# Written issue order on four engines for four column chunks of the first layer, and sliding attention in smaller steps

## The chip, the cores and the metric

The kernel runs on one NeuronCore of a Trainium2 chip. The core has a matrix engine (PE, with its weight loads shown as PEld), a vector engine (DVE), an activation engine (ACT), a general engine (POOL) and a queue engine (SP) that issues the DMA transfers here. The engines run beside each other; each takes its own instructions in order, and semaphores make one wait for another. The metric is device time in microseconds (us), the median of several executions; a profile is one execution, taken apart by the hardware profiler.

## What is computed

Two layers of a hybrid block on a sequence of 256 tokens (two blocks of 128, called t = 0 and t = 1) with 1024 channels, all in float32:

```
h = rms_norm(x)
z = h @ w_in                 # retention, conv, gated MLP, sliding attention and gate columns
ya = retention(za);  yb = conformer_conv(zb)
yc = spatial_gating(zc);  yd = swa_attention(zd)
mix = sum_b sigmoid(g_b) * (y_b @ w_branch[b])
x = x + mix @ w_out
x = x + swiglu(rms_norm(x))
```

The sliding attention has 8 query heads of width 64 that share 2 key and value heads. A token sees the 128 latest tokens, so block 0 meets 128 keys and block 1 meets 256. Scores get a bias and a sink term, then a softmax, then the product with the values.

## The kernel before

**Products.** Weights come in units of 2 x 128 x 1024 numbers, each half by one DMA (`load`, L121) into one of six buffers. `part` splits a half into a rounded main part `wh` (a cast on ACT, L129) and the rest `wl` (a subtraction on DVE, L130); there is room for four units of each. `mm` then does three matrix products per block of 128 rows: L152 (main by main), L153 (main by rest), L154 (rest by main). One column chunk (`chunk`) is 512 columns of `w_in` for both token blocks: two units, hence two half chunks of 24 products each. Taking the units of a chunk (`take`, `ahead`) first writes out the cast and subtraction of the units up to two ahead.

**PSUM.** Products of chunks go to four `acc` banks, everything else (transposes, scores, attention output) to four `mid` banks. A bank comes free when ACT or DVE has read it.

**Side work in steps.** The mixers are generators. `spawn` runs one to its first `yield`; `tick`, called after each half chunk, runs each waiting generator to its next `yield`. So side work is written into the program between half chunks of products. Below, T1, T2, ... are the ticks of `columns`, counted in each layer: chunk `pa` (first half of the convolution input) has T1 and T2, `pg` (its gate) T3 and T4, `pq` (retention queries) T5 and T6, `pk` (keys) T7 and T8, `pv` T9 and T10.

**Sliding attention.** For a token block: `swa_sums` (squares on ACT L460 and L461, sums on DVE, the inverse root on POOL L205), `swa_scaled` (DVE L475, L481), `swa_qkT` (transposes on PE L188 and L493, a copy of the queries on ACT L495, of the keys on DVE L496), `swa_soft` (score products L513; bias and row maximum on DVE L520 to L530; eight exponentials on ACT L534 with their sums; sum and reciprocal on DVE L537, L538; eight scalings on ACT L540), `swa_pT` (eight transposes L547 and two ACT copies L550 for one key block), `swa_pv` (L557) and `emit_y` (ACT L195, DVE L197). In the first layer, scores, scaling and transposes of block 0's queries up to `swa_qkT` are already done in `opening`.

**Order.** Instructions outside `manual_schedule` are put in order by a list scheduler that goes by its own estimates of time; inside it, the engines named take theirs in the order of the program. `opening` names PE, ACT, DVE and POOL (`ORDERED`). In `columns`, of either layer, the chunks `pa` to `pv` name PE alone. SP is never named; single DMAs are pinned to program order.

Of the kernel before, what the change touches and what calls it, by code (L numbers as in the profile page):

```python
# [2 lines left out]

# [5 lines left out]
F32 = mybir.dt.float32  # L9
BF16 = mybir.dt.bfloat16  # L10
F32R = mybir.dt.float32r
AF = mybir.ActivationFunctionType
# [4 lines left out]
P = 128  # L17
D = 1024
T = 2
# [63 lines left out]
class Kernel:  # L83
# [414 lines left out]
        )  # L498
        self.sqT[t] = qT

    def swa_soft(self, t):
        nc = self.nc
        nk = P * (t + 1)
        b0 = 256 - nk
        sc = self.b8.tile([P, 8, nk], F32, tag="b8", name="sc")
        mx = self.small("mx", 8)
        qT = self.sqT[t]
        for j0 in (0, 2):
            banks = [self.bank() for _ in range(2)]
            for j in (j0, j0 + 1):  # L510
                for v in range(2):
                    r = slice(64 * v, 64 * v + 64)
                    nc.tensor.matmul(  # L513
                        banks[v][:, (j - j0) * nk : (j - j0 + 1) * nk],
                        qT[r, j * P : (j + 1) * P], self.skT[r, 0:nk], start=True, stop=True,
                    )
            for j in (j0, j0 + 1):
                for v in range(2):
                    h = 4 * v + j
                    nc.vector.tensor_tensor_reduce(  # L520
                        out=sc[:, h, :], in0=banks[v][:, (j - j0) * nk : (j - j0 + 1) * nk],
                        in1=self.bias[:, h, b0:256], scale=1.0, scalar=NEG,
                        op0=ALU.add, op1=ALU.max, accum_out=mx[:, h : h + 1],
                    )
        nm = self.small("nm", 8)
        sk = self.col[:, C_SK : C_SK + 8]
        nc.vector.tensor_tensor(out=mx, in0=mx, in1=sk, op=ALU.max)
        nc.vector.tensor_scalar(out=nm, in0=mx, scalar1=-1.0, scalar2=None, op0=ALU.mult)
        es = self.small("es", 8)
        nc.vector.tensor_tensor(out=es, in0=sk, in1=mx, op=ALU.subtract)  # L530
        nc.scalar.activation(es, es, AF.Exp)
        den = self.small("den", 8)
        for h in range(8):
            nc.scalar.activation(  # L534
                sc[:, h, :], sc[:, h, :], AF.Exp, bias=nm[:, h : h + 1], accum_out=den[:, h : h + 1]
            )
        nc.vector.tensor_tensor(out=den, in0=den, in1=es, op=ALU.add)  # L537
        nc.vector.reciprocal(den, den)  # L538
        for h in range(8):
            nc.scalar.activation(sc[:, h, :], sc[:, h, :], AF.Copy, scale=den[:, h : h + 1])  # L540
        return sc

    def swa_pT(self, sc, pT, kb):
        for h0 in (0, 4):
# [189 lines left out]
                op0=ALU.add, op1=ALU.mult,  # L734
            )

    def chunk(self, act, pool=None):
        units = self.take(2)
        ps = [self.abank() for _ in range(T)]
        for i, u in enumerate(units):  # L740
            for t in range(T):
                self.cols(act, t, [u], ps[t], 4 * i)
            self.tick()
        return ps

# [9 lines left out]
        for _ in gen:  # L755
            pass

    def swa_task(self, t, psq, pskv, first=False):
        if not (first and t == 0):
            qk = self.swa_scaled(t, psq, pskv, *self.swa_sums(t, psq, pskv))  # L760
            for _ in range(1 + t):
                yield
            self.swa_qkT(t, *qk)
        yield
        sc = self.swa_soft(t)
        for _ in range(2 if first or t == 0 else 3):
            yield
        pT = self.b8.tile([P, t + 1, 8, P], F32, tag="b8", name="pT")
        self.swa_pT(sc, pT, 0)
        yield  # L770
        if t:
            self.swa_pT(sc, pT, 1)
            yield
        self.emit_y(3, t, self.swa_pv(t, pT), 1.0)

    def emit_y(self, b, t, src, scale):
# [2 lines left out]
        self.Y[b, t] = self.yt[b][:, t]  # L779
        self.split(self.Y[b, t], 0, src, scale)  # L780

    def conv_task(self, pa, pg):
        us = [self.conv_gate(pa[t], pg[t]) for t in range(T)]
        yield
        for t in range(T):
            self.conv_uT(t, us[t])
        yield
        k = 0
        per = TAP_PLAN
        for n in per:  # L790
            self.conv_taps(k, k + n)
            k += n
            yield
        st = [self.conv_norm(t) for t in range(T)]
        yield
        cn = [self.conv_scale(*st[t]) for t in range(T)]
        yield
        for t in range(T):
            self.conv_act(t, cn[t])

    def rot_task(self, ps, i):
        rs = [self.rotary(t, ps[t]) for t in range(T)]
        yield
        for t in range(T):
            pt = self.transpose4(rs[t])
            self.nc.scalar.copy(self.rqk[:, i, :, t * P : (t + 1) * P], pt.rearrange("p (h m) -> p h m", h=4))
# [30 lines left out]
    def columns(self, l, h0, h1_late, ready=None):  # L837
        nc = self.nc
        self.Y, self.yt, tasks = {}, {}, {}
        hT = [h0, h1_late]  # L840
        if not ready:
            self.swa_tiles()
            uq, ukv = self.take(2), self.take(1, 1)
        for t in range(T):
            if ready:
                psq, pskv = ready[t]
            else:
                psq, pskv = self.abank(), self.abank()
                self.cols(hT, t, uq, psq)
                if t == 0:  # L850
                    hT[1] = h1_late()
                self.cols(hT, t, ukv, pskv)
            tasks[3, t] = self.spawn(self.swa_task(t, psq, pskv, bool(ready)))
        if ready:
            self.bias_table()
        with self.tc.manual_schedule(engines={mybir.EngineType.PE}):
            self.ahead(self.pos + 2)
            pa = self.chunk(hT)
            pg = self.chunk(hT)
            if ready:  # L860
                self.constants()
            tasks[1] = self.spawn(self.conv_task(pa, pg))
            pq = self.chunk(hT)
            if ready:
                self.layer_rows(0)
            self.rqk = self.b8.tile([P, 2, 4, T * P], F32, tag="b8", name="rqk")
            tq = self.spawn(self.rot_task(pq, 0))
            pk = self.chunk(hT)
            tk = self.spawn(self.rot_task(pk, 1))
            pv = self.chunk(hT)  # L870
        self.rv, self.rg, self.gv = {}, {}, {}
        for t in range(T):
            self.rv[t] = self.work("rv")
            nc.scalar.copy(self.rv[t], pv[t])
        pg = self.chunk(hT)
        tasks[0] = self.spawn(self.ret_task(pg))
        pv = self.chunk(hT)
        tv = self.spawn(self.gv_task(pv))
        pu = self.chunk(hT)
        tasks[2] = self.spawn(self.gm_task(pu))  # L880
        need = {3: [tasks[3, 0], tasks[3, 1]], 0: [tasks[0]], 2: [tasks[2]], 1: [tasks[1]]}
        return hT, need
# [191 lines left out]
ORDERED = {  # L1074
    mybir.EngineType.PE, mybir.EngineType.Activation, mybir.EngineType.DVE, mybir.EngineType.Pool
}
# [86 lines left out]
```

## Time and profile before

| | us |
|---|---|
| median of three executions | 962.84 |
| lowest, highest | 961.56, 963.25 |
| profiled execution, device time | 963.32 |
| its span, first to last instruction | 961.3 |
| PE busy in the span | 951.0 |
| DVE busy | 707.3 |
| ACT busy | 504.6 |

Two us of the profiled execution lie outside the span, and its device time is 0.48 us above the median. PE is counted as busy from a product's start to its modelled end, also when the product runs at a lower clock; a wait of PE shows as idle time, and its releaser is the instruction that ended the wait. The column chunks of the first layer run from 30.1 us on, those of the second from about 506 us.

### The profile page before, as it was taken

To read this page: it belongs to the slowest core of one execution; us is meant where nothing else is said; L and a number is where in the kernel's file an instruction comes from. 1 tells how busy PE (TensorE), PEld (TensorE's weight loads), DVE (VectorE), ACT (ScalarE), POOL (GpSimd) and SP (SyncE) were. 2 spreads that over 40 slices of the span, in tenths; PEclk is the share of its full clock that TensorE was granted. 3 is DMA by queue.
4 is the path that set the end of the run, shared out by engine and by line. 5 is a ranking of instruction groups with operands and counts; after the bars stand their busy time and mean duration, and the time that the engine had idled before them with its cause. 6 is when DMAs were issued, how large, how long until landed. Compare 5 with 4: busy or idle time off the path is not lost.

```text
span 961.3 us, 12704 instructions
## 1 busy us (share of the span) xinstructions
PE 951.0 (99%) x4688; PEld 791.4 (82%) x4688; DVE 707.3 (74%) x1122; ACT 504.6 (52%) x756; POOL 38.9 (4%) x39
## 2 busy tenths in 40 slices
PE   8989999999999999999999999999999999999998
PEld 5867888888888888888887778888888888888886
DVE  6559999995767667656576699999766677566562
ACT  6486554445645555455466854545445555545540
POOL 1100020000100001000011000100010000000000
PEclk9999999999999999999999999999999999999999
DMA  9754636565555657655546366456655357556631
GB/s 330 242 213 154 220 131 189 186 199 193 174 176 175 206 177 256 199 191 180 176 141 214 107 197 198 154 183 190 199 180 190 111 186 249 191 185 196 191 96 44
DMA packets 50074, 177.01 MB, mean 184 GB/s; under 512 B 5563, under 2 KB 7132, under 8 KB 49884
## 3 DMA queue, kind: packets, MB, share of 16 engines
q1 hardware_dynamic: 49824, 176.07, 56.4%
q8 instruction: 37, 0.61, 0.3%
q14 instruction: 25, 0.20, 0.1%
q10 hardware_dynamic: 188, 0.12, 0.1%
HBM read 174.93 MB, written 1.25 MB: 183 GB/s over the span
## 4 chain that ended last, share of the span: by engine, by line
PE 94%; ACT 3%; DVE 1%; DMA 0%; issue 0%; POOL 0%; SPq 0%; DVEq 0%
PE acc L152 21%; PE acc L154 21%; PE acc L153 21%; PE mid L220 14%; PE mid L225 7%; PE mid L188 3%; PE mid L154 2%; PE mid L153 2%; PE mid L152 2%; PE acc L160 1%; ACT sc L534 1%; ACT sc L540 1%; ACT wh L129 1%; DVE wl L130 0%; DMA x<-x 0%; PE mid L557 0%
## 5 line engine op out<-in xcount | busy, mean ns | idle before, releaser
L130 DVE TENSOR_TENSOR wl<-raw,wh 128x1024 fp32r<-128x1024 f32 x314 | 378.9, 1220 | 139.2 <-ACT wh L129 89.7
L129 ACT CAST wh<-raw 128x1024 fp32r<-128x1024 f32 x314 | 323.3, 1050 | 221.5 <-PE acc L154 140.6
L152 PE MATMUL acc<-wh,hT 128*128 128x512 f32 (+1 forms) x608 | 238.5, 392 | 0.0
L154 PE MATMUL acc<-wh,hT 128*128 128x512 f32 (+1 forms) x608 | 236.1, 388 | 0.0
L153 PE MATMUL acc<-wl,hT 128*128 128x512 f32 (+1 forms) x608 | 235.7, 388 | 0.0
L220 PE MATMUL mid<-hT,wh 128*128 128x512 f32 x576 | 144.1, 392 | 0.0
L152 PEld LDWEIGHTS acc<-wh,hT 128*128 128x128 f32 x608 | 114.7, 189 | 24.6 <-issue 1.5
L154 PEld LDWEIGHTS acc<-wh,hT 128*128 128x128 f32 x608 | 114.6, 188 | 24.0 <-DVE hT L199 0.6
L153 PEld LDWEIGHTS acc<-wl,hT 128*128 128x128 f32 x608 | 114.7, 189 | 22.2
L220 PEld LDWEIGHTS mid<-hT,wh 128*128 128x128 f32 x576 | 104.2, 189 | 19.0
L152 PE MATMUL acc<-wh,yT 128*128 128x512 f32 x304 | 118.9, 391 | 0.0
L153 PE MATMUL acc<-wl,yT 128*128 128x512 f32 x304 | 118.4, 389 | 0.0
L154 PE MATMUL acc<-wh,yT 128*128 128x512 f32 x304 | 118.3, 389 | 0.0
L587 DVE SCALAR_TENSOR_TENSOR ca<-uT,col,ca 128x256 f32<-128x256 f32 x240 | 100.2, 477 | 0.0
L225 PEld LDWEIGHTS mid<-hT,wl 128*128 128x128 f32 x576 | 78.6, 190 | 5.6
L225 PE MATMUL mid<-hT,wl 128*128 128x256 f32 x576 | 80.3, 282 | 0.0
L154 PEld LDWEIGHTS acc<-wh,yT 128*128 128x128 f32 x304 | 57.1, 188 | 11.9
L152 PEld LDWEIGHTS acc<-wh,yT 128*128 128x128 f32 x304 | 57.1, 188 | 11.4
L153 PEld LDWEIGHTS acc<-wl,yT 128*128 128x128 f32 x304 | 57.1, 188 | 11.4
L890 ACT ACTIVATE gth<-acc 128x512 f32<-128x512 f32 x32 | 19.1, 597 | 31.0 <-PE acc L154 31.0
L205 POOL TENSOR_TENSOR rs<-rs,nhalf 128x1 f32<-128x1 f32 (+1 forms) x12 | 15.5, 1296 | 372.4 <-DVE rs L602 369.6
L234 ACT COPY fu<-mid 128x256 f32<-128x256 f32 x36 | 13.2, 368 | 31.1 <-PE mid L225 31.1
(172 smaller groups left out, 760.2 us busy)
## 6 DMA issues: line engine op xcount, KB each, us to landing
raw<-wu SPq DMA_DIRECT2D x320, 512.0 KB, 4.1
rows<-rows SPq DMA_DIRECT2D x2, 768.0 KB, 6.6
ng<-norms SPq DMA_DIRECT2D x3, 512.0 KB, 5.7
const<-const SPq DMA_DIRECT2D x1, 1088.0 KB, 7.9
bias<-rd SPq DMA_DIRECT2D x8, 128.0 KB, 7.6
out<-x SPq DMA_DIRECT2D x4, 256.0 KB, 2.1
x<-x SPq DMA_DIRECT2D x2, 256.0 KB, 3.7
x<-x SPq DMA_DIRECT2D x1, 512.0 KB
```

Of the source, the lines that this page charges most:

```text
L129: nc.scalar.copy(h, src)
L130: nc.vector.tensor_tensor(out=lo, in0=src, in1=h.bitcast(F32), op=ALU.subtract)
L152: nc.tensor.matmul(ps, xh, hs, start=start, stop=False)
L153: nc.tensor.matmul(ps, xh, ls, start=False, stop=False)
L154: nc.tensor.matmul(ps, xl, hs, start=False, stop=stop)
L188: self.nc.tensor.transpose(ps[:, b * P : (b + 1) * P], src[:, b * P : (b + 1) * P], self.ident)
L205: self.nc.gpsimd.tensor_tensor(out=out, in0=v, in1=self.nhalf[:, :n], op=ALU.pow)
L220: self.nc.tensor.matmul(ps.rearrange("p (s t m) -> p s t m", s=2, t=T), block(0, k), self.hT[:, :, :, k, :].rearrange("p t s m -> p s t m" ...
L225: self.nc.tensor.matmul(ps[:, : T * P].rearrange("p (t m) -> p t m", t=T), block(1, k), self.hT[:, :, 0, k, :], start=False, stop=k == kb - 1,
L234: self.nc.scalar.copy(out, low)
L587: nc.vector.scalar_tensor_tensor(out=self.ca[:, c, :], in0=self.uT[:, c, k : k + T * P], scalar=w[:, c, k : k + 1], in1=self.ca[:, c, :], ...
L890: self.nc.scalar.activation(th[t, n], ps[t], AF.Tanh, scale=0.5)
```

## The change

In the first layer (`ready` is set), the start of the attention, the bias table and the chunks `pa`, `pg`, `pq`, `pk` stand in `manual_schedule` with all four engines of `ORDERED`. In the second layer they stand in none, so that the list scheduler orders PE's instructions too. The chunk `pv` leaves the block in both layers.

`swa_soft` is cut into `swa_scores` (products, bias, maximum), `swa_exp` (exponentials, sums, reciprocal) and `swa_share` (scalings). No instruction is added, left out or made smaller. The first layer gets its own generator, and its two tasks are reversed, so that block 1's step stands ahead of block 0's at each tick. `conv_gate` of a token block is written right behind that block's last product of `pg` by a callback of `chunk`, where before both stood behind the chunk. Convolution and the retention queries wait one tick longer in the first layer.

| step | first layer, before | first layer, after | second layer, before | second layer, after |
|---|---|---|---|---|
| scaling, block 1 | start | T1 | start | start |
| scores, block 0 | T1 | T1 | T2 | T2 |
| exponentials, block 0 | T1 | T1 | T2 | T2 |
| transposes of queries and keys, block 1 | T2 | T2 | T2 | T3 |
| shares, block 0 | T1 | T2 | T2 | T2 |
| transposes of shares, block 0 | T3 | T3 | T4 | T5 |
| scores, block 1 | T3 | T4 | T3 | T4 |
| exponentials, block 1 | T3 | T5 | T3 | T4 |
| output, block 0 | T4 | T5 | T5 | T6 |
| shares, block 1 | T3 | T6 | T3 | T4 |
| transposes of the gated convolution input | T5 | T6 | T5 | T5 |
| transposes of shares, block 1 | T5, T6 | T7, T8 | T6, T7 | T6, T7 |
| transposes of retention queries | T7 | T8 | T7 | T7 |
| output, block 1 | T7 | T9 | T8 | T8 |

```diff
-    def swa_soft(self, t):
+    def swa_scores(self, t):
...
         nc.vector.tensor_tensor(out=es, in0=sk, in1=mx, op=ALU.subtract)
+        return sc, nm, es
+
+    def swa_exp(self, sc, nm, es):
+        nc = self.nc
         nc.scalar.activation(es, es, AF.Exp)
...
         nc.vector.reciprocal(den, den)
+        return den
+
+    def swa_share(self, st, den):
+        sc = st[0]
         for h in range(8):
-            nc.scalar.activation(sc[:, h, :], sc[:, h, :], AF.Copy, scale=den[:, h : h + 1])
-        return sc
+            self.nc.scalar.activation(sc[:, h, :], sc[:, h, :], AF.Copy, scale=den[:, h : h + 1])
...
-    def chunk(self, act, pool=None):
+    def chunk(self, act, done=None):
...
                 self.cols(act, t, [u], ps[t], 4 * i)
+                if i and done:
+                    done(t, ps[t])
             self.tick()
...
+    def swa_task(self, t, psq, pskv):
+        qk = self.swa_scaled(t, psq, pskv, *self.swa_sums(t, psq, pskv))
+        for _ in range(3 if t else 1):
+            yield
+        self.swa_qkT(t, *qk)
+        yield
+        st = self.swa_scores(t)
+        self.swa_share(st, self.swa_exp(*st))
+        for _ in range(2 if t else 3):
             yield
...
+    def first_swa_task(self, t, psq, pskv):
+        if t:
+            sums = self.swa_sums(t, psq, pskv)
+            yield
+            qk = self.swa_scaled(t, psq, pskv, *sums)
+            yield
+            self.swa_qkT(t, *qk)
+            yield
+        yield
+        st = self.swa_scores(t)
+        if t:
+            yield
+        den = self.swa_exp(*st)
+        yield
+        self.swa_share(st, den)
+        yield
+        pT = self.b8.tile([P, t + 1, 8, P], F32, tag="b8", name="pT")
+        self.swa_pT(st[0], pT, 0)
+        yield
+        if t:
+            self.swa_pT(st[0], pT, 1)
+        yield
         self.emit_y(3, t, self.swa_pv(t, pT), 1.0)
...
-        with self.tc.manual_schedule(engines={mybir.EngineType.PE}):
+        with self.tc.manual_schedule(engines=ORDERED) if ready else nullcontext():
+            for t in range(T):
...
+                tasks[3, t] = self.spawn((self.first_swa_task if ready else self.swa_task)(t, psq, pskv))
             if ready:
+                self.tasks.reverse()
+            if ready:
+                self.bias_table()
             self.ahead(self.pos + 2)
             pa = self.chunk(hT)
-            pg = self.chunk(hT)
+            us = []
+            self.chunk(hT, lambda t, ps: us.append(self.conv_gate(pa[t], ps)))
...
-            tk = self.spawn(self.rot_task(pk, 1))
-            pv = self.chunk(hT)
+            tk = self.spawn(self.rot_task(pk, 1, False))
+        pv = self.chunk(hT)
```

More of the change, by code (lines that the diff above doesn't have):

```diff
@@ L1 @@
 import math
-from contextlib import ExitStack
+from contextlib import ExitStack, nullcontext
 import concourse.bass as bass
@@ L756, in finish @@
             pass
[L758 to L763, printed above, removed]
+    def swa_task(self, t, psq, pskv):
[3 more added lines that the diff above has]
+        self.swa_qkT(t, *qk)
         yield
-        sc = self.swa_soft(t)
-        for _ in range(2 if first or t == 0 else 3):
+        st = self.swa_scores(t)
+        self.swa_share(st, self.swa_exp(*st))
+        for _ in range(2 if t else 3):
             yield
         pT = self.b8.tile([P, t + 1, 8, P], F32, tag="b8", name="pT")
-        self.swa_pT(sc, pT, 0)
+        self.swa_pT(st[0], pT, 0)
         yield
         if t:
-            self.swa_pT(sc, pT, 1)
+            self.swa_pT(st[0], pT, 1)
             yield
+        self.emit_y(3, t, self.swa_pv(t, pT), 1.0)
+    def first_swa_task(self, t, psq, pskv):
[15 more added lines that the diff above has]
+        pT = self.b8.tile([P, t + 1, 8, P], F32, tag="b8", name="pT")
+        self.swa_pT(st[0], pT, 0)
+        yield
+        if t:
+            self.swa_pT(st[0], pT, 1)
+        yield
         self.emit_y(3, t, self.swa_pv(t, pT), 1.0)
@@ L780, in emit_y, with conv_task @@
         self.split(self.Y[b, t], 0, src, scale)
-    def conv_task(self, pa, pg):
-        us = [self.conv_gate(pa[t], pg[t]) for t in range(T)]
+    def conv_task(self, us, first):
         yield
+        if first:
+            yield
         for t in range(T):
@@ L799, in conv_task, with rot_task @@
             self.conv_act(t, cn[t])
-    def rot_task(self, ps, i):
+    def rot_task(self, ps, i, first):
         rs = [self.rotary(t, ps[t]) for t in range(T)]
         yield
+        if first:
+            yield
         for t in range(T):
@@ L843, in columns @@
             uq, ukv = self.take(2), self.take(1, 1)
-        for t in range(T):
-            if ready:
[L846 to L855, printed above, removed]
-        with self.tc.manual_schedule(engines={mybir.EngineType.PE}):
+        with self.tc.manual_schedule(engines=ORDERED) if ready else nullcontext():
+            for t in range(T):
+                if ready:
+                    psq, pskv = ready[t]
+                else:
+                    psq, pskv = self.abank(), self.abank()
+                    self.cols(hT, t, uq, psq)
+                    if t == 0:
+                        hT[1] = h1_late()
+                    self.cols(hT, t, ukv, pskv)
+                tasks[3, t] = self.spawn((self.first_swa_task if ready else self.swa_task)(t, psq, pskv))
+            if ready:
+                self.tasks.reverse()
+            if ready:
+                self.bias_table()
             self.ahead(self.pos + 2)
             pa = self.chunk(hT)
-            pg = self.chunk(hT)
+            us = []
+            self.chunk(hT, lambda t, ps: us.append(self.conv_gate(pa[t], ps)))
             if ready:
                 self.constants()
-            tasks[1] = self.spawn(self.conv_task(pa, pg))
+            tasks[1] = self.spawn(self.conv_task(us, bool(ready)))
             pq = self.chunk(hT)
@@ L866, in columns @@
             self.rqk = self.b8.tile([P, 2, 4, T * P], F32, tag="b8", name="rqk")
-            tq = self.spawn(self.rot_task(pq, 0))
+            tq = self.spawn(self.rot_task(pq, 0, bool(ready)))
             pk = self.chunk(hT)
-            tk = self.spawn(self.rot_task(pk, 1))
-            pv = self.chunk(hT)
+            tk = self.spawn(self.rot_task(pk, 1, False))
+        pv = self.chunk(hT)
         self.rv, self.rg, self.gv = {}, {}, {}
```

## The prediction

> **What bounds the kernel now.** I read the page first, then the list of who waited for whom, then PE's timeline where the waits lie, and last the timelines of the engines named as releasers.
>
> ```profile
> span 961.3 us, 12704 instructions
> ## 1 busy us (share of the span) xinstructions
> PE 951.0 (99%) x4688; PEld 791.4 (82%) x4688; DVE 707.3 (74%) x1122; ACT 504.6 (52%) x756; POOL 38.9 (4%) x39
> ```
>
> PE is busy for 951.0 of 961.3 us. No reordering takes products away, so what can be won is PE's idle time and what it loses by running slowly. PE's waits of the stretch 42.8 to 60 us (first layer) and of 490 to 570 us (second layer) are these:
>
> ```profile
> PE mid L513 <- ACT pT L550: 1.9, 1, 1.9
> PE mid L547 <- ACT sc L540: 0.8, 1, 0.8
> ```
>
> ```profile
> PE mid L188 <- DVE mx L520: 0.6, 1, 0.6
> PE mid L188 <- DVE cvu L567: 0.2, 1, 0.2
> ```
>
> These rows count only time in which PE ran nothing. Single steps inside a group also start late, so I go by starts in PE's timeline. First layer (start, duration, engine, line, operation):
>
> ```profile
> 42.77 0.27 PE L493 MATMUL mid<-first,kn 128*128 128x128 f32 x1
> ...
> 49.34 2.37 PE L547 MATMUL mid<-first,sc 128*128 128x128 f32 x8 [0.82 <-ACT sc L540]
> 51.64 1.14 PE L513 MATMUL mid<-skT,swqT 64*128 64x256 f32 x8
> ...
> 63.50 1.08 PE L557 MATMUL mid<-pT,sv 128*64 128x512 f32 x4
> ...
> 70.10 1.79 PE L547 MATMUL mid<-first,sc 128*128 128x128 f32 x8
> 71.72 1.04 PE L188 MATMUL mid<-first,cvu 128*128 128x128 f32 x8
> ...
> 78.08 1.04 PE L547 MATMUL mid<-first,sc 128*128 128x128 f32 x8
> 78.87 0.48 PE L152 MATMUL acc<-wh,hT 128*128 128x512 f32 x1
> ```
>
> Second layer, the scores of block 1 and the next transposes of shares:
>
> ```profile
> 525.40 2.00 PE L513 MATMUL mid<-skT,swqT 64*128 64x256 f32 x16
> ...
> 532.95 1.03 PE L547 MATMUL mid<-first,sc 128*128 128x128 f32 x8
> ```
>
> Now the same work can be compared where it waits and where it doesn't.
> - 24 products and 8 transposes: 42.77 to 51.64 is 8.87 us; undisturbed, 71.72 to 78.08, it is 6.36. Lost: 2.51.
> - 16 score products and 24 products: 51.64 to 63.50 is 11.86; in the second layer, 525.40 to 532.95, it is 7.55. Lost: 4.31.
> - 8 transposes: 70.10 to 71.72 is 1.62; 78.08 to 78.87 is 0.79. Lost: 0.83.
>
> Together 7.65 us, more than the 2.7 us of waits. Part of the rest is the clock, in the first row of the stretches asked for here:
>
> ```profile
> 56.70:60.00 3.30, 3.30 (x10) 2.56 (x9) 3.06 (x14) 0.31 (x1) 0.00 (x0) 0.50 0.95 379
> 80.00:200.00 120.00, 120.00 (x571) 99.44 (x570) 118.22 (x223) 59.19 (x77) 6.20 (x4) 1.00 0.56 181
> ```
>
> From 56.7 to 60.0 the granted clock is 0.50, right behind the stall: half of 3.3 us, 1.65 us, is lost there, inside the 4.31. The Trainium skill, "TensorE: Matmul & The Clock Gate", section "Part 1: The HAM clock gate", says that the clock is halved after about one idle window of 3.4 us and that the low state lasts for at least such a window. The trace agrees in the length of the slow stretch, and shows that a stall broken up by single transposes is enough.
>
> Why PE waits there is in ACT's timeline:
>
> ```profile
> 30.48 0.26 ACT L468 COPY sv<-acc 128x128 f32<-128x128 f32 x1
> ...
> 42.97 0.59 ACT L495 COPY swqT<-mid 128x512 f32<-128x512 f32 x1 [9.96 <-PE mid L188]
> ...
> 44.75 0.21 ACT L531 ACTIVATE es<-es 128x8 f32<-128x8 f32 x1 [0.23 <-DVE es L530]
> ...
> 48.88 2.44 ACT L540 ACTIVATE sc<-sc,den 128x128 f32<-128x128 f32 x8
> 51.23 2.92 ACT L129 CAST wh<-raw 128x1024 fp32r<-128x1024 f32 x3
> 54.06 1.05 ACT L550 COPY pT<-mid 128x512 f32<-128x512 f32 x2
> ```
>
> ACT stands still for 9.96 us in front of the copy of block 1's queries, which PE produces only at T2, while block 0's exponentials sit behind it with their scores long computed. They begin at 44.75, the shares are done after 51.2, and PE had asked for them at 48.3. Three casts then go ahead of the copies at 54.06 that free the `mid` banks for the scores of block 1. So the stall is a matter of order, not of work.
>
> **The change part by part.** It adds no instruction and removes none; it moves them. I walk through the written order of the first layer, from these rows of DVE and from ACT's above:
>
> ```profile
> 27.07 3.49 DVE L130 TENSOR_TENSOR wl<-raw,wh 128x1024 fp32r<-128x1024 f32 x3
> ...
> 48.08 0.17 DVE L537 TENSOR_TENSOR den<-den,es 128x8 f32<-128x8 f32 x1 [2.23 <-ACT sc L534]
> ```
>
> ```profile
> L520 DVE CUSTOM_DVE_ANT_0 sc<-mid,bias 128x256 f32<-128x256 f32 x8 | 2.8, 418 | 0.0
> L520 DVE CUSTOM_DVE_ANT_0 sc<-mid,bias 128x128 f32<-128x128 f32 x8 | 1.8, 287 | 0.5 <-PE mid L513 0.5
> L475 DVE TENSOR_TENSOR swqn<-acc,swrs 128x512 f32<-128x512 f32 x2 | 1.4, 692 | 2.9 <-POOL swrs L205 2.9
> ```
>
> *Casts and subtractions (units 4 to 6) ahead of everything.* In written order six casts follow block 1's value copy at 30.48 to 30.74. One takes 0.97 us (2.92 / 3), so ACT is done at 36.6. The six subtractions at 1.16 us (3.49 / 3) follow the first cast and end at 31.7 + 7.0 = 38.7. PE needs unit 4 after 36.8 and unit 5 after 42.8: covered, by 2.7 us for unit 4. The price if that cover were gone is one for one on PE.
>
> *T1, block 0's scores and exponentials.* DVE: scaling of block 1 about 1.0 (0.69 for the queries, the keys a quarter of their size), scores 1.8, the small steps about 0.5: done at 42.0. ACT: exponentials from then on, which with their sums take 48.08 - 44.75 = 3.33, to 45.3; the reciprocal about 0.3 more. The scaling of block 1 is done at 39.7, ahead of PE's transposes at T2 (42.3).
>
> *T2, shares.* ACT copies the queries meanwhile (0.6), then eight scalings in 2.44 us: done at about 48.1. PE comes to the eight transposes at 42.77 + 5.57 = 48.3, and to the last of them 0.7 us later. This is the tightest place: 0.2 us for all of them, about 1 us for the last. I take it as no wait; the other end is 1 to 2 us if my estimates of the small steps are short.
>
> *T3 and T4.* Four casts (units 7 and 8, 3.9 us) and the two copies of transposes (1.05) stand next on ACT: done at 53.1. PE reaches the scores of block 1 at 48.3 + 6.36 = 54.7 and wants the `mid` banks: 1.6 us of cover, where before it waited 1.92 us. These casts need their data. The transfers are issued when the subtractions of units 4 and 5 free the buffers, the last at about 36.3, which is later than before; the row on the buffers between 31 and 50 us gives the time to land:
>
> ```profile
> DMA to landing us min/median/max: 4.5/4.9/5.3
> ```
>
> So the last lands at about 42, against 48 to 52 for the casts. On SP's queue the constants and unit 9 stand behind them and move too; unit 9 is wanted after 69.
>
> *The convolution gate inside the chunk* reads its PSUM banks at about 53.5 and 55.6, ahead of `pq`, which wants one `acc` bank at 54.7 + 1.9 = 56.6 and the second 2.8 us later. Cover 2 to 3 us.
>
> *T5 to T9.* Exponentials of block 1 end near 64, its shares near 68, and PE transposes them only after 75: seven us of cover. The output of block 1 comes two ticks later, but its branch product is first wanted after all eight chunks. Convolution starts a tick later: its 120 tap instructions and DVE are spoken of below.
>
> So the first layer gains all of 7.65 us, if every cover above holds.
>
> *Second layer.* The transposes of block 1's queries go to a tick of their own (T3), so they no longer meet the scores of block 0 in the four `mid` banks: the 0.58 to 0.6 us wait on L520 goes. The earlier gate takes away the 0.2 us wait on L567. PE's order is now the scheduler's; elsewhere the list shows no wait of PE in stretches that it already ordered (99 to 490 us, from `pv` on). The bounds are a gain of 0.8 and, if the scheduler misjudges a step, a loss of about one first-layer wait, 1.9. I take a gain of 0.6, nearest to the two wait rows.
>
> Sum: 963.32 - 7.65 - 0.6 = 955.1 for the profiled execution. It lay 0.5 us above the median of 962.84, so the median should come to **954.6**.
>
> **The rivals.**
>
> *A rest of the stall stays.* The shares come 1 to 2 us late at T3, or a bank at T4. By the clock row, a short stall may bring 1.65 us of half clock with it. That leaves 3.4 to 6.4 us of the 8.2: 956.5 to 959.5. For it: 0.2 us of cover at T3 rests on small steps that I estimated. Against it: the last transposes have 1 us. The clock rule of the page named above, taken by itself, would leave a stall below 3.4 us at full clock, and this rival would then end 1.65 us lower.
>
> *DVE becomes the bound and the gain is given back.* In the second row of the stretches, DVE is busy for 118.2 of 120 us between 80 and 200, and its work would now have 7.65 us less. If PE had to wait for that, the time would be 962.2, no change. Against it: the wait list has no wait of PE on DVE there, and from 200 to 240 DVE has time to catch up. The Trainium skill, "Perfetto Trace Analysis", section "Optimizing Scalar/DVE Operations", advises smaller pieces where these engines hold up others without being saturated. Here pieces keep their size and only their order changes, and DVE is nearly saturated later on; the row above is why I keep this rival.
>
> *Slower: a cast blocks ACT in written order.* Before, the scheduler put casts where it thought the data was there; now four casts stand in front of the copies and the gate at T3. If unit 8 lands late, the `mid` banks stay full and PE waits one for one. It decides from a landing at about 52 + 1.6 = 53.6 on, and makes the kernel slower by over 0.2% (1.9 us) once the landing comes after 53.6 + 8.2 + 1.9 = 63.7. At a landing at 65 the time would be 966. By the landing row it is 42. The Trainium skill, "PSUM — Partial Sum Buffer", section "Engine vs sequencer instructions", says that the queues of ACT and DVE are strictly first in, first out; the trace agrees, with 9.96 us in which ACT held a cast behind the copy. This rule speaks against writing out the order, and for a small chance of this rival.
>
> **How the numbers follow.** The forecast, 953.6 to 956.2, has 0.66; the rest of the stall, 956.2 to 960.5, 0.18; the gain given back 0.07; slower 0.09. The range 953.4 to 960.5 takes in the first two, 0.84; its low end is the median less the whole 8.45 us (7.65 + 0.8) and one us for the spread of the runs. A measurement of this kernel can tell about 0.2%, 1.9 us, from no change. Faster by more than that: 0.84; within: 0.07; slower: 0.09.
>
> **What would show it.** In the new profile PE should have no wait on L540 or L550 in the first 90 us, a clock of 1.00 from 50 to 65, and block 0's transposes of shares near 48.3 with block 1's scores behind the next 24 products, near 54.7. ACT's long idle should end with the exponentials near 42, not with the query copy. In the second layer the wait on L520 should be gone. I am wrong if PE still waits at T3 or T4, if DVE's subtractions become a releaser of PE between 80 and 200, or if casts wait for transfers around 48 to 52.

## The result and the profile after

The changed kernel takes 955.1 us (median), the kernel before 963.0 in the same comparison; the ratio is 0.992, with a 95% interval of 0.9901 to 0.994. That is 7.9 us less, where 8.2 were forecast. The profiled execution took 954.92 us with a span of 953.0. A fourth execution of the changed kernel took 3870 us, for a reason that is not on record, and is left out below.

The page of the new kernel, its head:

```profile
span 953.0 us, 12691 instructions
## 1 busy us (share of the span) xinstructions
PE 947.1 (99%) x4688; PEld 789.7 (83%) x4688; DVE 708.4 (74%) x1122; ACT 504.4 (53%) x756; POOL 38.3 (4%) x39
```

The engines do the same work as before (4688 matrix instructions, DVE 708.4 against 707.3 us). The span is 8.3 us shorter. PE's list of waits over the whole execution has only two rows left, both in the opening (columns: total us, times, longest):

```profile
PE mid L314 <- DVE warm L309: 1.2, 1, 1.2
PE acc L160 <- DVE wl L327: 0.4, 1, 0.4
```

PE's timeline in the first layer, without the products (new line numbers: L554 is the transposes of shares, L564 the output):

```profile
42.73 0.27 PE L493 MATMUL mid<-first,kn 128*128 128x128 f32 x1
...
48.33 1.03 PE L554 MATMUL mid<-first,sc 128*128 128x128 f32 x8
...
54.76 2.00 PE L513 MATMUL mid<-skT,swqT 64*128 64x256 f32 x16
...
62.39 1.08 PE L564 MATMUL mid<-pT,sv 128*64 128x512 f32 x4
```

Block 0's transposes start at 48.33 (49.34 before), as one unbroken group of eight. From them to the scores of block 1 it is 6.43 us for 8 transposes and 24 products, and from those scores to the output of block 0 7.63 us, where it was 11.86 for the same 40 instructions. ACT's timeline shows why (L535 and L538 the exponentials, L548 the shares, L557 the copies of transposes):

```profile
30.59 5.79 ACT L129 CAST wh<-raw 128x1024 fp32r<-128x1024 f32 x6
41.57 0.21 ACT L535 ACTIVATE es<-es 128x8 f32<-128x8 f32 x1 [5.19 <-DVE es L530]
...
44.77 0.56 ACT L495 COPY swqT<-mid 128x512 f32<-128x512 f32 x1
45.40 2.45 ACT L548 ACTIVATE sc<-sc,den 128x128 f32<-128x128 f32 x8
47.75 3.88 ACT L129 CAST wh<-raw 128x1024 fp32r<-128x1024 f32 x4
51.53 1.06 ACT L557 COPY pT<-mid 128x512 f32<-128x512 f32 x2
```

The idle time of 10 us in front of the query copy has become 5.2 us in front of the exponentials. They start 3.2 us sooner, and no cast stands between them and the shares. In PE's clock the slow stretch is gone (window, span, busy time of PE, PEld, DVE, ACT, POOL, clock, DMA share, GB/s):

```profile
50.00:65.00 15.00, 15.00 (x73) 11.08 (x72) 13.48 (x30) 12.13 (x28) 1.29 (x1) 1.00 0.77 269
```

In the second layer the transposes of block 1's queries stand by themselves, 24 products behind the scores of block 0, and nothing is waited for:

```profile
510.20 1.16 PE L513 MATMUL mid<-skT,swqT 64*128 64x128 f32 x16
...
516.87 0.60 PE L188 MATMUL mid<-first,swqn 128*128 128x128 f32 x4
```

### The profile page after: what moved, and what is told of

It is laid out like the page before. It is cut to its first block, busy times and chain, and to the rows that moved or that the text cites. A ratio compares the mean times of both kernels' runs of the same rounds, so it can differ in the third digit from the quotient of the medians.

```text
span 953.0 us, 12691 instructions
## 1 busy us (share of the span) xinstructions
PE 947.1 (99%) x4688; PEld 789.7 (83%) x4688; DVE 708.4 (74%) x1122; ACT 504.4 (53%) x756; POOL 38.3 (4%) x39
## 4 chain that ended last, share of the span: by engine, by line
PE 98%; DMA 0%; DVE 0%; ACT 0%; issue 0%; POOL 0%; SPq 0%; DVEq 0%
PE acc L152 22%; PE acc L154 22%; PE acc L153 22%; PE mid L220 14%; PE mid L225 7%; PE mid L188 3%; PE mid L152 2%; PE mid L154 2%; PE mid L153 2%; PE acc L160 1%; PE mid L513 1%; PE mid L564 1%; PE mid L554 1%; DMA x<-x 0%; PE mid L736 0%; PE mid L684 0%
## 5 line engine op out<-in xcount | busy, mean ns | idle before, releaser
L152 PEld LDWEIGHTS acc<-wh,yT 128*128 128x128 f32 x304 | 57.1, 188 | 11.5
```

Source lines behind the costliest of these rows:

```text
L152: nc.tensor.matmul(ps, xh, hs, start=start, stop=False)
```

## The experiments

The theory: the time before was lost to the order in which ACT and DVE handed PE its inputs and banks, in two places that add up, and PE takes each delay one for one once a measured cover is used up. The rivals are those of the prediction, and that one half of the change does it all. Edits are against the changed kernel. Its time is 955.1 us throughout; the kernel before had a median of 963.0 to 963.3 us in each of the four comparisons.

**The two layers apart.** `first_only` gives the second layer its old steps, its old gates and PE's fixed order:

```diff
-        for _ in range(3 if t else 1):
+        for _ in range(1 + t):
...
-        for _ in range(2 if t else 3):
+        for _ in range(3 if t else 2):
...
+        with self.tc.manual_schedule(engines=ORDERED if ready else {mybir.EngineType.PE}):
```

> First layer as changed, second layer as it was before. Theory (two independent gains on PE's path): the first layer keeps its 7.3 us, the second layer gives its 1.0 us back, so 955.1 + 1.0 = 956.1 us. Rival (the second layer's new freedom for the scheduler does nothing by itself, and all comes from the first layer): 955.1 us.

`second_only` gives the first layer back all that it had before (its task, PE alone in order, gates behind the chunk):

```diff
+        with self.tc.manual_schedule(engines={mybir.EngineType.PE}) if ready else nullcontext():
...
+        self.swa_share(st, self.swa_exp(*st))
+        for _ in range(2):
             yield
```

> First layer as it was before, second layer as changed. Theory: 963.0 - 1.0 = 962.0 us, with PE's waits of 1.9 and 0.8 us and the half clock of the first layer still there. Rival: 963.0 us.

`first_only` took 955.86 us, `second_only` 962.36, the kernel before 963.17 in that comparison. So the first layer alone is worth 7.3 us and the second 0.8; taken off again from the changed kernel the second is worth 0.76. The two add up. The gain of `second_only` by itself is not clear of the noise (ratio 0.9993, interval 0.9984 to 1.0003), but its executions fall into the same three groups as those of the kernel before (see the last section), each 0.8 us lower. Its profile has lost the waits on L520 and on the gate, and in `first_only` these two are the only ones that are back:

```profile
PE mid L188 <- DVE mx L520: 0.6, 1, 0.6
PE mid L188 <- DVE cvu L574: 0.2, 1, 0.2
```

Which part of the second layer's change (the moved steps, the earlier gate, the scheduler's order on PE) took away which wait was not separated.

**Steps without written order.** `steps_only` names PE alone in the first layer:

```diff
-        with self.tc.manual_schedule(engines=ORDERED) if ready else nullcontext():
+        with self.tc.manual_schedule(engines={mybir.EngineType.PE}) if ready else nullcontext():
```

> All of the change, but in the first layer only PE is issued as written; ACT, DVE and POOL are ordered by the list scheduler as before. Theory (the order on ACT makes block 0's shares late, the smaller steps keep block 1's scores away from the full banks): the 2.5 us at the transposes of block 0's shares come back, the 4.3 us behind them do not, so 957.6 us, or 959.2 if a half clock of 1.65 us follows the stall. Rival 1 (the written order does all of it): 962 us. Rival 2 (the smaller steps do all of it): 955.1 us.

Measured: 957.38 us, ratio 0.9939 (0.9924 to 0.9954). The list scheduler brings back the old order on ACT up to T3, and PE's first stall is back, but not the second:

```profile
42.95 0.59 ACT L495 COPY swqT<-mid 128x512 f32<-128x512 f32 x1 [10.65 <-PE mid L188]
43.44 1.06 ACT L129 CAST wh<-raw 128x1024 fp32r<-128x1024 f32 x1
44.73 0.21 ACT L535 ACTIVATE es<-es 128x8 f32<-128x8 f32 x1 [0.23 <-DVE es L530]
```

```profile
49.31 2.37 PE L554 MATMUL mid<-first,sc 128*128 128x128 f32 x8 [0.81 <-ACT sc L548]
...
57.11 2.00 PE L513 MATMUL mid<-skT,swqT 64*128 64x256 f32 x16
```

The shares are late as before, while block 1's scores, now a half chunk later, find their banks free. On top of the steps the written order is worth 2.3 us (957.38 - 955.1), so the steps by themselves give 5.0 of the first layer's 7.3. Which of the moved steps gives how much was not taken apart further.

**Written order without the steps.** `order_only` keeps all four engines in order, with the coarse steps of before and the gates behind the chunk:

```diff
         st = self.swa_scores(t)
-        if t:
-            yield
-        den = self.swa_exp(*st)
-        yield
-        self.swa_share(st, den)
-        yield
+        self.swa_share(st, self.swa_exp(*st))
+        for _ in range(2):
+            yield
```

> The first layer has all four engines issued as written, but with the coarse steps of before (exponentials and shares in one step, block 1's scores in the tick of block 0's transposes, convolution gates behind the chunk). Theory: block 1's scores wait for the banks behind four casts on ACT (about 4.5 us and a half clock of 1.65), and the gates stand behind block 1's softmax on ACT, so that the next chunk waits for its banks (up to 5.6 us): 962 to 969 us, no better than before. Rival (the written order is what wins): 955 to 957 us.

Measured: 966.38 us, ratio 1.0032 (1.0022 to 1.0041): slower than the kernel before by 3.2 us. Its second layer is the changed one, so against `second_only`, which differs in the first layer alone, the loss is 4.0 us. The profile is of the fastest execution (964.73 us). There PE waits in the two places that were named, and for 6.7 us the clock is halved:

```profile
PE mid L513 <- ACT pT L557: 3.1, 1, 3.1
PE acc L152 <- ACT cvth L572: 3.1, 1, 3.1
```

```profile
52.40:59.10 6.70, 4.97 (x14) 3.71 (x15) 6.17 (x22) 2.58 (x6) 0.00 (x0) 0.50 0.80 281
```

So this was the slower side of the same change: an order written out on engines that take their instructions strictly in turn is only as good as the steps in it.

**The cover at T3.** `exp_late` writes block 0's exponentials behind the copy of block 1's queries:

```diff
         st = self.swa_scores(t)
+        yield
+        den = self.swa_exp(*st)
         if t:
             yield
-        den = self.swa_exp(*st)
-        yield
         self.swa_share(st, den)
```

> The changed kernel, with block 0's exponentials written behind the copy of block 1's queries (T2), where the old order had them. Theory (PE takes each share's transpose when it is ready): shares run 47.3 to 49.7 us instead of 45.4 to 47.9, the last transpose goes from 49.0 to 49.8, so PE loses 0.8 us: 955.9 us, with no half clock. Rival (this one place was the whole cause of the old stall): 959 to 963 us.

`delay6` and `delay12` put idle work on DVE between the scores and the exponentials of block 0:

```diff
+        else:
+            pad = self.work("pad")
+            self.nc.vector.memset(pad, 0.0)
+            for _ in range(6):
+                self.nc.vector.tensor_scalar(out=pad, in0=pad, scalar1=1.0, scalar2=None, op0=ALU.mult)
+            self.nc.vector.tensor_scalar(
+                out=st[1], in0=st[1], scalar1=pad[:, 0:1], scalar2=None, op0=ALU.add
+            )
         den = self.swa_exp(*st)
```

The tile is zero, so the results stay what they are.

> The changed kernel with six extra multiplications by 1.0 of a scratch tile on DVE, about 3.0 us, between the scores and the exponentials of block 0. Theory (cover of about 1.1 us at the last transpose of T3, then one for one): PE loses 1.9 us, 957.0 us at full clock. Rival (a stall this short already halves the clock, 1.65 us): 958.6 us.

> The same with twelve, about 5.6 us. Theory (one for one behind the cover): PE loses 4.5 us, 959.6 us at full clock; with a half clock behind it, 961.2 us. Rival (a first cover of some us elsewhere takes it up): 955 to 957 us.

`exp_late`: 955.7 us. The 0.8 us expected are 0.7, inside PE's group of eight (1.75 us against 1.03):

```profile
48.33 1.75 PE L554 MATMUL mid<-first,sc 128*128 128x128 f32 x8
```

So the place of the exponentials on ACT alone was not the old stall, of which 2.5 us lay in front of these transposes. In the kernel before, DVE held them back too. Its copy of block 1's keys had waited 4.70 us for PE, and behind it, after a subtraction of weights, came the small step (L530) that the exponentials needed:

```profile
43.08 0.35 DVE L496 TENSOR_SCALAR skT<-mid,derived 128x128 f32<-128x128 f32 x1 [4.70 <-PE mid L493]
43.35 0.16 DVE L528 TENSOR_SCALAR nm<-mx 128x8 f32<-128x8 f32 x1
43.42 1.22 DVE L130 TENSOR_TENSOR wl<-raw,wh 128x1024 fp32r<-128x1024 f32 x1
44.56 0.16 DVE L530 TENSOR_TENSOR es<-col,mx 128x8 f32<-128x8 f32 x1
```

A cast then stood ahead of the shares and three ahead of the copies. That these together make up the rest is read from the rows; no run moves them one by one.

`delay6`: 958.28 us, the profiled execution 957.57. The extra work, by DVE's timeline, delays the exponentials by 3.5 us: one 0.48 us fill, then

```profile
42.19 2.74 DVE L801 TENSOR_SCALAR pad<-pad 128x512 f32<-128x512 f32 x6
44.96 0.23 DVE L802 TENSOR_SCALAR nm<-nm,pad 128x8 f32<-128x8 f32 x1
```

and PE comes to the next steps at

```profile
49.41 2.38 PE L554 MATMUL mid<-first,sc 128*128 128x128 f32 x8 [0.85 <-ACT sc L548]
...
57.21 2.00 PE L513 MATMUL mid<-skT,swqT 64*128 64x256 f32 x16
```

that is 2.45 us later than in the changed kernel (57.21 against 54.76), 0.08 of it from before 42.8. The cover is 3.5 - 2.4, about 1.1 us, near the 1 that was forecast for the last transpose. Two executions ran as the theory says (957.4 and 957.6 us, with 3.5 us of extra work in place of 3.0), and two as the rival says (959.0 and 959.2).

`delay12` took 961.39 us, its profiled execution 960.91. The shares come 6.2 us later than in the changed kernel (51.64 against 45.40) and the scores of block 1 5.8 us later (60.56 against 54.76):

```profile
51.64 2.45 ACT L548 ACTIVATE sc<-sc,den 128x128 f32<-128x128 f32 x8
```

```profile
60.56 2.00 PE L513 MATMUL mid<-skT,swqT 64*128 64x256 f32 x16
```

Less the cover of 1.1, one for one gives 5.1, and about 0.7 us are left to a stretch of half clock; from the transposes to the scores it is 8.46 us, against 7.80 in `delay6`. The stretch starts among the transposes that wait for their shares, and costs less than the 1.65 us of the expectation. That the total of 961.2 was met is in part luck, since the extra work was longer (6.2 us, not 5.6) and the half clock cheaper:

```profile
52.30:55.60 3.30, 3.30 (x11) 2.35 (x11) 0.54 (x1) 3.30 (x9) 0.00 (x0) 0.50 0.01 2
```

**The gates.** `gate_late` writes the first layer's gates behind the chunk, after block 1's scores:

```diff
-            self.chunk(hT, lambda t, ps: us.append(self.conv_gate(pa[t], ps)))
+            if ready:
+                pg = self.chunk(hT)
+                us = [self.conv_gate(pa[t], pg[t]) for t in range(T)]
```

> The changed kernel with the first layer's convolution gates written behind the chunk again, after the scores of block 1. Theory (DVE then handles 2.8 us of scores ahead of the gates, and the next chunk waits for its acc bank from 56.7 to about 59.4 us): PE loses 2.8 us, 957.9 us, or 959.5 with a half clock. Rival (the gates' place does not matter): 955.1 us.

Measured: 955.03 us, no change; the expectation was wrong. DVE does the gates' product late, as foreseen, and PE does not care:

```profile
59.08 1.28 DVE L574 SCALAR_TENSOR_TENSOR cvu<-cvth,acc 128x512 f32<-128x512 f32 x2
```

The product reads the first half's banks. The gate's own banks are read by the tanh on ACT alone, which ran at 52.42 and 54.78 here, so they were free for `pq`, which PE started at 56.6. In `order_only` it was this tanh that PE waited for.

**Late transfers.** `late_load` fetches the constants three times in a row ahead of units 7 and 8:

```diff
+            if ready:
+                self.constants()
+                for _ in range(2):
+                    self.pin(self.nc.sync.dma_start(out=self.const, in_=self.a["const"]))
```

> The changed kernel with the table of constants fetched three times in a row ahead of units 7 and 8 on SP's queue, so that these land later: by my estimate at 52 to 58 us in place of about 42. Theory (cover of the casts up to a landing at 53.6, then one for one): the last landing less 53.6 us is what PE loses in front of block 1's scores, 0 to 5 us: 955 to 960 us. Rival (a blocked cast on ACT costs little, since the other engines go on): 955.1 us whatever the landing.

Measured: 954.72 us. The casts of units 7 and 8 now wait for their data:

```profile
48.14 1.05 ACT L129 CAST wh<-raw 128x1024 fp32r<-128x1024 f32 x1 [0.37 <-DMA raw<-wu]
49.41 2.25 ACT L129 CAST wh<-raw 128x1024 fp32r<-128x1024 f32 x2 [0.22 <-DMA raw<-wu]
51.82 1.05 ACT L129 CAST wh<-raw 128x1024 fp32r<-128x1024 f32 x1 [0.17 <-DMA raw<-wu]
```

The last landed at about 51.8, ten us after the estimate for the changed kernel, and still inside the cover. This bears out the cover up to there. A landing behind 53.6 was not reached, so the price beyond it stays untried, and the run does not tell theory and rival apart. Why it ran 0.4 us shorter than the changed kernel was not followed up.

**DVE, full from 80 to 200.** `dve_pad4` puts four small operations into each tick from T9 on:

```diff
+        if 9 <= self.count < 30:
+            for _ in range(4):
+                self.nc.vector.scalar_tensor_tensor(
+                    out=self.pad, in0=self.pad, scalar=1.0, in1=self.pad, op0=ALU.mult, op1=ALU.max
+                )
```

> The changed kernel with four extra small operations on DVE in each tick from T9 to T29 of the first layer, 84 in all, some 17 to 24 us of DVE time in the stretch where it is busy for 118.7 of 120 us. Theory (the taps of the convolution have room, so DVE is full there but binds nothing): 955.1 us. Rival (DVE is the bound behind PE, with little room): 965 to 975 us.

It took 971.3 us and says nothing on that stretch. The operations depend on nothing, and the list scheduler moved all 84 ahead: 44 into the opening, where PE lost 2.5 us, and 40 in between the written instructions, in front of block 0's scores:

```profile
39.67 13.02 DVE L767 SCALAR_TENSOR_TENSOR pad<-pad 128x128 f32<-128x128 f32 x40
```

```profile
PE mid L188 <- DVE mx L520: 11.5, 1, 11.5
```

What it does show is that these 13 us on DVE cost PE 14.2 us: block 0's transposes of shares start at 65.02 in place of 48.33, less the 2.5 us of the opening. Of that 11.5 us are a wait of PE, and behind it, from 56 to 60 us, the clock is 0.50. `taps_pad2` and `taps_pad4` tie the extra operations to what each convolution tap has just written:

```diff
+            if self.extra:
+                for c in range(2):
+                    nc.vector.scalar_tensor_tensor(
+                        out=self.pad, in0=self.ca[:, c, :P], scalar=1.0, in1=self.pad, op0=ALU.mult, op1=ALU.max
+                    )
```

> The changed kernel with two extra operations on DVE behind every tap of the first layer's convolution, each reading what that tap wrote, so that they can't be moved ahead: 60 in all, at 0.33 us 20 us more DVE work between 78 and 210 us, where DVE is full. Theory (DVE is full there but the taps have room: the last ends at 209 us and PE transposes the sum at 237): 955.1 us. Rival (DVE is the bound behind PE): about 975 us.

> The same with four per tap, 120 in all, 39 us. Theory: 27 us of room and some us of idle time on DVE take up most of it; the rest, up to 10 us, may show: 955 to 965 us. Rival: about 994 us.

`taps_pad2`: 954.94 us, no change. DVE's windows, 80 to 200 and 200 to 240:

```profile
80.00:200.00 120.00, 120.00 (x575) 99.58 (x574) 118.68 (x250) 61.04 (x79) 4.39 (x4) 1.00 0.56 182
200.00:240.00 40.00, 40.00 (x183) 33.19 (x182) 39.97 (x75) 16.94 (x18) 0.00 (x0) 1.00 0.61 193
```

In the changed kernel the second of them is

```profile
200.00:240.00 40.00, 40.00 (x182) 33.21 (x181) 28.50 (x37) 16.94 (x18) 0.00 (x0) 1.00 0.61 192
```

DVE was full to 200 and stays so (118.68 of 120); the extra work comes out behind 200, where DVE goes from 28.50 to 39.97 of 40, and PE's share does not move. Over the whole execution DVE is busy for 720.0 us, against 708.4: one operation takes 0.28 us but overlaps the next, so the 60 add 11.6 us, and not the 20 of the expectation. `taps_pad4` took 960.45 us, and there PE waits at last, on the gated sums that DVE takes from PE's banks (L947):

```profile
PE acc L152 <- DVE gth L947: 2.2, 1, 2.2
```

The 120 operations add 23.3 us to DVE's busy time and cost 5.4. So DVE has room for 60 of these operations and not for 120.

## Why the prediction was right

*What bounds the kernel.* PE's path, as read. The stall was put down to ACT's order alone; DVE's rows under `exp_late` show the same fault there, with the exponentials' last input behind a copy that waited for PE. "Their scores long computed" holds for the scores (38.2 us), not for that input (44.7). 7.65 us were counted as lost in the first layer by comparing the starts of equal work; by itself the first layer gave 7.3. The list of waits would have given 2.7. The difference is transposes that trickle in one by one and products at half clock, neither of which counts as idle.

*The sum.* 955.1 for the profiled execution, measured 954.92; 954.6 for the median, measured 955.1. The term for the second layer was mis-sized: 0.6 was taken from the rows of waits, and 0.76 to 0.8 were measured. The method of the first layer would have come out too high there: by starts of equal work the two places come to 0.68 and 0.38 us, and the expectations for the two runs said 1.0.

*The walk through the written order.* Six subtractions to end at 38.7 (they did at 38.6), exponentials from 42.0 (41.57), shares done at 48.1 (47.85), copies of transposes at 53.1 (52.6). The 0.4 us on DVE are a sum of small overestimates, half of it in the scaling of block 1 (0.8 us, not 1.0). The cover at T3 was 0.5 us for all transposes and 1.1 for the last, against 0.2 and 1, and `delay6` measured it.

*The gate's cover* was read from the wrong instruction. The step said that the convolution gate frees the banks at 53.5 and 55.6, 2 to 3 us ahead of `pq`. The bank that `pq` needs is freed by the tanh; the product can be 5 us later for nothing. With the first layer's new steps the callback in `chunk` bought no time.

*A rest of the stall stays:* it did not, but `delay6` shows how near it was, 1.1 us, and that a half clock may come with it, as priced.

*DVE as the bound:* wrong, with room for at least 11.6 us by `taps_pad2`; the 23.3 us of `taps_pad4` use it up.

*A cast that blocks ACT:* not here. `order_only` shows a like mechanism, with gates and copies behind other work on ACT, and it ends slower than before. The price of a cast that waits for its transfer past the cover was not measured.

*The clock.* The 1.65 us of half clock were part of the gain in the median. Where the kernel before ran at a clock of 0.999 (961.6 us), the gain is 6.5 us; less 0.8 for the second layer that is 5.7, against 7.65 - 1.65 = 6.0 by the prediction's count. That the median of the kernel before falls where it does is luck for the gain of 7.9, not for the time of 955.1.

## What to carry to other kernels

Price a stall by comparing the starts of equal work where it runs freely, not by the idle time of the bound engine: here 7.3 us were to be had where the waits said 2.7. Writing out the order of in-order engines and cutting the side work into steps that fit between blocks of products belong together: of the first layer's 7.3 us the steps alone gave 5.0, and the order alone lost 4.0. An engine that is 99% busy need not be a bound: look for how long its last results lie before they are used.

## What was not expected of the hardware

The half clock is not there in every execution. Over the three comparisons of the experiments the kernel before ran in three groups: ten executions at 961.5 to 961.8 us with a mean clock of 0.999, most at 963.0 to 963.4 with 0.996 or 0.998, and eleven at 964.3 to 964.7 with 0.995 or 0.996. `second_only`, which keeps the stall, has the same groups: 960.9 with 1.0, 962.3 with 0.998, 963.4 to 963.9 with 0.996. The steps are about 1.4 us, and half of a slow stretch of 3.3 us is 1.65. So the same stall seems to bring none, one or two such stretches. This is not shown: each kernel has a trace of one execution only, with one stretch in that of the kernel before, and a clock of 0.996 in the middle group does not fit one stretch. The changed kernel's three other executions lie between 954.92 and 955.12, with a clock of 1.0.

`delay6`, whose PE loses 2.4 us in pieces, ran at 957.4 and 957.6 with a clock of 0.999 and at 959.0 and 959.2 with 0.998. The trace, of 957.57, has a clock of 1.00 from 40 to 70 us; that the two others had a slow stretch there is read from their time and mean clock. The Trainium skill, "TensorE: Matmul & The Clock Gate", section "Part 1: The HAM clock gate", halves the clock after about one idle window of 3.4 us, on windows that run freely. The free window fits the scatter. The length of idle time that it asks for does not fit the trace of the kernel before, if it means one unbroken gap: the longest idle time of PE that it shows ahead of the slow stretch is 1.92 us. Without the stall, the kernel lost its scatter together with its 8 us.
